# One number in a planner's table: the high half of a piece of the input is ranked earlier in the opening of a transformer block

## The chip, the core and the metric

The kernel runs on one core of a Trainium2 chip. A core has a matrix engine (TensorE, here PE), a vector engine (VectorE, DVE), an engine for activations and copies (ScalarE, ACT), a general one (GpSimd, POOL) and one that here only issues transfers (SyncE, SP). Each works through its own list of instructions in order and waits for the others by semaphores. The metric is the device time of one execution in microseconds, as the median of several runs.

## The reference

A decoder block on 1024 rows of 1024 channels. The opening of the kernel computes the part from `x` to the queries and keys: each row is scaled by the reciprocal root of its mean square, each channel by a gain, and the result is multiplied by the columns of `w_in` that make q and k.

```
def hybrid_layer(h, ..., w_in, ..., mix_pre_g, ...):
    u = rms_norm(h, mix_pre_g)
    z = jnp.einsum('bsd,de->bse', u, w_in)
    p, q, k, v = z[..., :o1], z[..., o1:o2], z[..., o2:o3], z[..., o3:o4]
    gate_a, gate_b = z[..., o4:o5], z[..., o5:]
    ya = pool_mixer(p, ...) @ w_branch_a
    yb = diff_attention(q, k, v, ...) @ w_branch_b
    m = sigmoid(gate_a) * ya + sigmoid(gate_b) * yb
    h = h + rms_norm(m @ w_out, mix_post_g)
    u = rms_norm(h, ffn_pre_g)
    f = silu(u @ w_ffn_gate) * (u @ w_ffn_up)
    return h + rms_norm(f @ w_ffn_down, ffn_post_g)
```

## The kernel before

**Numbers in two halves.** Every matrix operand is split into a high half, its rounding to the matrix engine's format, and a low half, the value minus that rounding. A product is then three matmuls: high by high, high by low, low by high. In most places ACT makes the high half (a CAST row) and DVE the low half (a TENSOR_TENSOR row of line 1405).

**The input in quarters.** The normalised input is kept transposed, channels along the partitions, in four quarters of 512 channels by 512 rows of `x`: A11 and A12 hold rows 0 to 511, A21 and A22 rows 512 to 1023; the second digit of A11/A12 is the channel half. A11 and A12 are prepared in two pieces, rows 0 to 255 and rows 256 to 511. A21 lies in the buffer S1_raw and A22 in S3_raw until sums overwrite them. In names without buffer numbers A11, A12, A21 and A22 are all just `A`, and S1_raw and S3_raw are `S_raw`.

A piece goes through these steps. Line 430 on ACT (or 433 on DVE) scales by the gain, in place or from the loaded buffer; a group of two blocks of 128 rows gets its sums of squares on ACT (line 389, "square"), a mean on DVE (397), a root on POOL (398), a transposition on PE that spreads it over the partitions (404) and a copy into the table `R` (408). Then follows the second stage, `second_stage(n, q, ii)`:

```
pl.op("DVE", dve(size), lambda: tt(a(), a(), Rs()[:, rest]..., ALU.mult), ..., rank=R + OFF[3], port=True)
e = HI[2 * n + q]
o = pl.op(e, act(size) ..., (A.copy ...)(hi2()[:, ks, c], a()), ..., rank=R + OFF[4], ...)
pl.op("DVE", dve(size), lambda: k.sub(lo2()[:, ks, c], a(), hi2()[:, ks, c]), ..., rank=R + OFF[5], port=True)
```

So: multiply by R on DVE (line 303), round on ACT or DVE (line 458, "the rounding"), subtract on DVE (line 1405). `n` is 0 and 1 for the two pieces of A11/A12 and 2 for A21/A22, and `q` the channel half. A21 is done in two halves of 1024 columns, A22 at once with 2048.

**What PE does meanwhile.** Heads 0 and 1 get queries and keys by plain matmuls (line 542): first over rows 0 to 255, then 256 to 511 (128x256 matmuls), then 512 to 1023 (128x512). Head 2 follows by a scheme of seven products (lines 1498 to 1500) on sums S1 to S4 of the quarters, which DVE forms from 2048-column rows, and on differences of the weights (wf_t at line 601, Wh and Wl at lines 591 and 1405). The finished queries and keys go through ACT and DVE (`qk_st`, the high half and the remainder) and out by SP. Fillers that keep PE busy before the first data (`warm`) come first. The rest of the kernel, from about 81 us on, is written in another order of code and its instructions are the same.

**What sets the order.** The opening is planned before anything is emitted. Each step is an operation with an engine, an estimated cost, its predecessors and a rank. `aim` gives each step a due time from the PE step that needs it, and adds the step's own rank to it; `schedule` then goes along the estimated time and gives each engine, of the steps that could start within a short patience (0.1 us for DVE and ACT, none for PE), the one with the lowest rank. On PE, a step that is not yet possible is passed over for one that is. Every later choice depends on the earlier ones. What comes out is a fixed list for each engine; on the chip nothing is reordered. The rank of a piece's steps is its entry in `XT` plus the entry in `OFF` for the kind of step; entry 2n + q belongs to the piece.

Of the kernel before, what the change touches and what calls it, by code (L numbers as in the profile page):

```python
# [257 lines left out]
UNS = ()  # L258
GROUPS = ((0, 1,), (2, 3,), (4, 5,), (6, 7,),)
RT = (10.633, 28.077, 18.684, 6.937,)  # L260
XT = (-25.843, 33.103, -24.124, -5.443, 51.062, -7.924,)
XG = ("DVS", "ACT", "ACT", "ACT", "ACT", "ACT",)
HI = ("ACT", "ACT", "DVE", "ACT", "ACT", "ACT",)
UHI = ("ACT", "ACT",)
# [16 lines left out]
def opening(pl, k):  # L281
# [57 lines left out]
    def pcols(n):  # L339
        return slice(2 * P * n, 2 * P * (n + 1)) if n < 2 else slice(None)  # L340
# [72 lines left out]
    def first_stage(n, q, ii):  # L413
        t = n // 2
        A_, ks, R = RAWS[t, q], slice(2 * ii[0], 2 * ii[-1] + 2), XT[2 * n + q] + .001 * ii[0]
        c, width, nk = pcols(n), 2 * P if t == 0 else HALF, 2 * len(ii)
# [27 lines left out]
    def second_stage(n, q, ii):  # L444
        t = n // 2
        A_, ks, R = RAWS[t, q], slice(2 * ii[0], 2 * ii[-1] + 2), XT[2 * n + q] + .001 * ii[0] + (LATE if n in UNS else 0)
        c, width, nk = pcols(n), 2 * P if t == 0 else HALF, 2 * len(ii)
# [1529 lines left out]
```

## Time and profile before

| | |
|---|---|
| median of 3 runs | 1242.33 us (1241.83 to 1242.55) |
| the profiled execution | 1242.02 us, its span 1240.2 us |
| PE busy | 1231.4 us of the span |
| DVE busy | 844.6 us |
| ACT busy | 584.1 us |
| POOL busy | 126.8 us |
| first 512-wide matmul, first matmul of head 2's scheme | 37.48 us, 59.26 us |

All times within the execution count from the start of the span. A row of the order in time gives start, duration, engine, line, operation, output and inputs, how many equal instructions were merged into it, and in square brackets how long the engine had been idle and whose work ended that. Instructions of one engine overlap a little: the next starts before the last has ended, so what an instruction costs its engine is the distance between two starts. The ends of matmuls are modelled; a busy PE can hide short waits. A row of stretches gives the length, then busy time and count for PE, PEld (weight loads), DVE, ACT and POOL, the granted clock, the share of the transfer engines and GB/s.

### The profile page before, as it was taken

Reading aid. Unit: us, or ns where it says so; the run is one execution under the profiler, and the core shown is the slowest. Engines: PE = TensorE matmul, PEld = TensorE weight load, DVE = VectorE, ACT = ScalarE, POOL = GpSimd, SP = SyncE. Lnnn points to the kernel's source line nnn. Section 1 sums busy time; section 2 is a strip of 40 time slices with the busy share of each in tenths; the row PEclk is TensorE's granted clock in tenths of the full one; section 3 lists DMA queues with packets and bytes.
Section 4 is the critical chain, followed back from the end, with each engine's and each line's share of the span. In section 5 each row is a group of like instructions: output and inputs, shape, how many; then the busy total and the mean of one; then the engine's idle time right before and its main releaser. Section 6 shows DMA issues by size and latency. Waiting matters only on the chain.

```text
span 1240.2 us, 15622 instructions
## 1 busy us (share of the span) xinstructions
PE 1231.4 (99%) x5860; PEld 1034.7 (83%) x5860; DVE 844.6 (68%) x1307; ACT 584.1 (47%) x1049; POOL 126.8 (10%) x108
## 2 busy tenths in 40 slices
PE   9999999999999999999999999999999999999998
PEld 9888888888899998888888888888888888888886
DVE  6986784544599888886885564565655548855666
ACT  8643443443587773454643333333333334454542
POOL 1000000000201110011001111101111101000222
PEclk9999999999999999999999999999999999999999
DMA  9665246423883028663523233232332468633236
GB/s 373 238 194 186 104 166 212 135 73 116 300 310 137 18 86 294 195 241 102 189 90 121 86 127 103 97 98 98 114 127 86 125 225 287 214 102 102 81 106 212
DMA packets 133820, 194.36 MB, mean 157 GB/s; under 512 B 7920, under 2 KB 82416, under 8 KB 131312
## 3 DMA queue, kind: packets, MB, share of 16 engines
q1 hardware_dynamic: 126928, 172.26, 41.5%
q10 hardware_dynamic: 6816, 21.11, 4.4%
q8 instruction: 46, 0.75, 0.2%
q14 instruction: 30, 0.25, 0.1%
HBM read 131.73 MB, written 61.60 MB: 156 GB/s over the span
## 4 chain that ended last, share of the span: by engine, by line
PE 95%; DMA 3%; DVE 1%; ACT 1%; SPq 0%; issue 0%; POOLq 0%; DVEq 0%; ACTq 0%
PE Y L1498 10%; PE Y L1499 10%; PE Y L1500 10%; PE X L1498 5%; PE X L1500 5%; PE X L1499 5%; PE Yd L1498 3%; PE Yd L1499 3%; PE Yd L1500 3%; PE Z L1500 3%; PE Z L1498 3%; PE Z L1499 3%; PE s L710 3%; PE o L710 3%; PE qk L542 3%; PE wo L1500 2%
## 5 line engine op out<-in xcount | busy, mean ns | idle before, releaser
L1449 DVE TENSOR_TENSOR p<-Z,p 128x512 f32<-128x512 f32 x32 | 22.1, 691 | 161.1 <-PE Z L1500 161.1
L1498 PE MATMUL X<-S_hi,Wh 128*128 128x512 f32 x288 | 112.5, 391 | 0.0
L1498 PE MATMUL Y<-S_hi,Wh 128*128 128x512 f32 x288 | 112.4, 390 | 0.0
L1499 PE MATMUL Y<-S_lo,Wh 128*128 128x512 f32 x288 | 112.3, 390 | 0.0
L1500 PE MATMUL Y<-S_hi,Wl 128*128 128x512 f32 x288 | 112.3, 390 | 0.0
L1500 PE MATMUL X<-S_hi,Wl 128*128 128x512 f32 x288 | 112.2, 390 | 0.0
L1499 PE MATMUL X<-S_lo,Wh 128*128 128x512 f32 x288 | 112.2, 390 | 0.0
L1498 PE MATMUL Y<-A_hi,Wh 128*128 128x512 f32 x280 | 109.2, 390 | 0.0
L1499 PE MATMUL Y<-A_lo,Wh 128*128 128x512 f32 x280 | 109.2, 390 | 0.0
L1500 PE MATMUL Y<-A_hi,Wl 128*128 128x512 f32 x280 | 109.1, 390 | 0.0
L1467 ACT CAST Wh<-wf_t 128x1024 fp32r<-128x1024 f32 x62 | 64.3, 1052 | 64.3 <-PE Y L1499 32.9
L1405 DVE TENSOR_TENSOR w_op<-wd,w_op 128x512 fp32r<-128x512 f32 x77 | 56.6, 735 | 53.3 <-ACT w_op L1453 53.2
L1405 DVE TENSOR_TENSOR Wl<-wf_t,Wh 128x1024 fp32r<-128x1024 f32 x72 | 87.6, 1224 | 6.1 <-ACT Wh L1467 4.6
L1453 ACT CAST w_op<-wd 128x512 fp32r<-128x512 f32 x77 | 47.9, 622 | 81.6 <-PE Yd L1500 36.2
L1467 ACT CAST Wh<-w_raw 128x1024 fp32r<-128x1024 f32 (+1 forms) x62 | 51.9, 837 | 63.1 <-PE Z L1499 38.3
L1405 DVE TENSOR_TENSOR Wl<-w_raw,Wh 128x1024 fp32r<-128x1024 f32 x72 | 68.7, 954 | 15.1 <-ACT Wh L1467 13.6
L1498 PE MATMUL Yd<-w_op,s_op 128*128 128x512 f32 x176 | 68.7, 390 | 0.0
L1499 PE MATMUL Yd<-w_op,s_op 128*128 128x512 f32 x176 | 68.6, 390 | 0.0
L1500 PE MATMUL Yd<-w_op,s_op 128*128 128x512 f32 x176 | 68.4, 390 | 0.0
L1498 PEld LDWEIGHTS Y<-S_hi,Wh 128*128 128x128 f32 x288 | 54.1, 188 | 11.6 <-ACT u L1540 0.5
L1500 PEld LDWEIGHTS X<-S_hi,Wl 128*128 128x128 f32 x288 | 54.1, 188 | 11.2
L1500 PEld LDWEIGHTS Y<-S_hi,Wl 128*128 128x128 f32 x288 | 54.1, 188 | 11.2
(294 smaller groups left out, 3025.8 us busy)
## 6 DMA issues: line engine op xcount, KB each, us to landing
s_raw<-fsd SPq DMA_DIRECT2D x35, 512.0 KB, 3.7
w_raw<-in_w_in_dram SPq DMA_DIRECT2D x24, 512.0 KB, 4.2
w_raw<-in_w_ffn_gate_dram SPq DMA_DIRECT2D x22, 512.0 KB, 3.9
w_raw<-in_w_ffn_up_dram SPq DMA_DIRECT2D x22, 512.0 KB, 3.9
fsd<-fss SPq DMA_DIRECT2D x11, 1024.0 KB, 3.9
wd<-in_w_ffn_down_dram SPq DMA_DIRECT2D x44, 256.0 KB, 5.4
fsd<-F SPq DMA_DIRECT2D x33, 256.0 KB, 2.4
sgs<-sgd SPq DMA_DIRECT2D x16, 512.0 KB, 8.5
```

Source lines behind the costliest of these rows:

```text
L542: nc.tensor.matmul(o()[:, cs], l, r, start=first and kk == 2 * kh and j == 0, stop=last and kk == 2 * kh + 1 and j == len(todo) - 1, skip_ ...
L710: nc.tensor.matmul(o, l, r, start=start, stop=stop, skip_group_check=skip)
L1405: nc.vector.tensor_tensor(out=o, in0=a, in1=f32(hi), op=ALU.subtract)
L1449: nc.vector.tensor_tensor(out=o, in0=a, in1=b, op=op)
L1453: nc.scalar.copy(hi, a)
L1467: nc.scalar.copy(hi, a)
L1498: nc.tensor.matmul(o, ah, bh, start=start, stop=False, skip_group_check=goes_on)
L1499: nc.tensor.matmul(o, ah, bl, start=False, stop=False, skip_group_check=goes_on)
L1500: nc.tensor.matmul(o, al, bh, start=False, stop=stop, skip_group_check=goes_on)
```

## The change

One entry of the table `XT` changes: the fourth, n = 1 and q = 1, which is A12's piece of rows 256 to 511. It is lowered by 16.

```
 RT = (10.633, 28.077, 18.684, 6.937,)
-XT = (-25.843, 33.103, -24.124, -5.443, 51.062, -7.924,)
+XT = (-25.843, 33.103, -24.124, -21.443, 51.062, -7.924)
 XG = ("DVS", "ACT", "ACT", "ACT", "ACT", "ACT",)
 HI = ("ACT", "ACT", "DVE", "ACT", "ACT", "ACT",)
```

All steps of that piece get a lower rank: its scaling on ACT, its multiplication, its rounding and its low half. The planner is run again, so everything behind the first different choice may come out otherwise. No instruction is added, removed or resized in the opening.

The lists are equal up to the third of four squares that run in a row on ACT. From there, ACT's list before (numbers behind a name are buffer numbers; `w_raw` are loaded weights, `gk` the gain):

```order
L389 ACTIVATE junk_79,ss_83_413<-xt_49_197 128x1024
L389 ACTIVATE junk_79,ss_83_413<-xt_52_207 128x1024
L458 CAST A12_hi_62_276<-A12_raw_50_199 128x4x256
L430 ACTIVATE S1_raw_53_214<-S1_raw_53_214,gk_36_138 128x512
L430 ACTIVATE S3_raw_55_223<-S3_raw_55_223,gk_36_138 128x512
L430 ACTIVATE S1_raw_53_214<-S1_raw_53_214,gk_36_138 128x512
L430 ACTIVATE S3_raw_55_223<-S3_raw_55_223,gk_36_138 128x512 x3
L515 ACTIVATE qk_st_90_497<-qk_67_297 128x512
```

And ACT's list now, at the same place:

```order
L389 ACTIVATE junk_79,ss_83_413<-xt_49_197 128x1024
L458 CAST A12_hi_62_276<-A12_raw_50_199 128x4x256
L389 ACTIVATE junk_79,ss_83_413<-xt_52_207 128x1024
L430 ACTIVATE S1_raw_53_214<-S1_raw_53_214,gk_36_138 128x512
L430 ACTIVATE S3_raw_55_223<-S3_raw_55_223,gk_36_138 128x512
L430 ACTIVATE S1_raw_53_214<-S1_raw_53_214,gk_36_138 128x512
L430 ACTIVATE S3_raw_55_223<-S3_raw_55_223,gk_36_138 128x512
L515 ACTIVATE qk_st_90_484<-qk_67_297 128x512
L430 ACTIVATE S3_raw_55_223<-S3_raw_55_223,gk_36_138 128x512
L430 ACTIVATE S1_raw_53_214<-S1_raw_53_214,gk_36_138 128x512
L430 ACTIVATE S3_raw_55_223<-S3_raw_55_223,gk_36_138 128x512
```

The rounding of A12's second piece has changed places with the last square; behind that, the last scaling of S3_raw has moved from the sixth place of its row to the eighth, with a qk rounding and a scaling of S1_raw in between.

PE's list where it reaches rows 256 to 511, before (`qk` are accumulators, `w_hi` and `w_lo` weights, `R` and `rstd` the roots' transposition):

```order
L542 MATMUL qk_67_297<-A11_hi_59_252,w_hi_63_280 128x256 x4
L542 MATMUL qk_60_262<-A11_hi_59_252,w_hi_58_239 128x256 x4
L542 MATMUL qk_77_358<-A11_hi_59_252,w_hi_71_323 128x256 x4
L542 MATMUL qk_80_375<-A11_hi_59_252,w_hi_73_331 128x256 x2
L404 MATMUL R_88_453<-ident_72,rstd_85_438 128x128 x2
L542 MATMUL qk_80_375<-A11_hi_59_252,w_hi_73_331 128x256 x2
L542 MATMUL qk_67_297<-A12_hi_62_276,w_hi_63_280 128x256 x2
L404 MATMUL R_89_462<-ident_72,rstd_87_449 128x128 x2
```

And PE's list now, at the same place:

```order
L542 MATMUL qk_67_297<-A11_hi_59_252,w_hi_63_280 128x256 x4
L542 MATMUL qk_60_262<-A11_hi_59_252,w_hi_58_239 128x256 x4
L542 MATMUL qk_67_297<-A12_hi_62_276,w_hi_63_280 128x256 x4
L542 MATMUL qk_67_297<-A11_hi_59_252,w_lo_68_300 128x256 x2
L404 MATMUL R_86_450<-ident_72,rstd_85_439 128x128 x2
L542 MATMUL qk_67_297<-A11_hi_59_252,w_lo_68_300 128x256 x2
L542 MATMUL qk_67_297<-A12_hi_62_276,w_lo_68_300 128x256 x4
L542 MATMUL qk_67_297<-A11_lo_64_282,w_hi_63_280 128x256 x4
L542 MATMUL qk_67_297<-A12_lo_69_313,w_hi_63_280 128x256 x4
L404 MATMUL R_89_476<-ident_72,rstd_88_466 128x128 x2
```

The first use of A12's second piece stands behind 8 matmuls of this part instead of 16; the eight for `qk_77` and `qk_80` come later. The second transposition stands behind all of `qk_67`.

DVE's list from the multiplication of S3_raw by R on, before (`A21_lo` and `A22_lo` are low halves; the second `S1_raw<-S1_raw,R` is A21's second half):

```order
L303 TENSOR_TENSOR S3_raw_55_223<-S3_raw_55_223,R_57_230 128x2048
L518 SCALAR_TENSOR_TENSOR qk_st_90_497<-qk_67_297,qk_st_90_497 128x512
L1405 TENSOR_TENSOR qk_st_93_525<-qk_60_262,qk_st_93_525 128x512
L601 TENSOR_TENSOR wf_t_95_543<-w_raw_78_368,w_raw_65_286 128x512
L601 TENSOR_TENSOR wf_t_95_543<-w_raw_78_368 128x512
L1405 TENSOR_TENSOR A21_lo_97_560<-S1_raw_53_214,A21_hi_91_504 128x1024
L518 SCALAR_TENSOR_TENSOR qk_st_96_556<-qk_77_358,qk_st_96_556 128x512
L303 TENSOR_TENSOR S1_raw_53_214<-S1_raw_53_214,R_57_230 128x1024
```

And DVE's list now:

```order
L518 SCALAR_TENSOR_TENSOR qk_st_90_484<-qk_67_297,qk_st_90_484 128x512
L303 TENSOR_TENSOR S3_raw_55_223<-S3_raw_55_223,R_57_230 128x2048
L1405 TENSOR_TENSOR qk_st_91_509<-qk_60_262,qk_st_91_509 128x512
L601 TENSOR_TENSOR wf_t_95_545<-w_raw_78_368,w_raw_65_286 128x512
L601 TENSOR_TENSOR wf_t_95_545<-w_raw_78_368 128x512
L518 SCALAR_TENSOR_TENSOR qk_st_96_549<-qk_77_358,qk_st_96_549 128x512
L1405 TENSOR_TENSOR A21_lo_98_571<-S1_raw_53_214,A21_hi_93_528 128x1024
L1405 TENSOR_TENSOR A22_lo_101_586<-S3_raw_55_223,A22_hi_97_562 128x2048
L1405 TENSOR_TENSOR qk_st_100_584<-qk_80_375,qk_st_100_584 128x512
L303 TENSOR_TENSOR S1_raw_53_214<-S1_raw_53_214,R_57_230 128x1024
```

A21's second multiplication now stands behind A22's low half of 2048 columns and one more qk remainder. Its rounding on ACT follows it in both, and PE's use of that rounding is the seventeenth 512-wide matmul in both lists. Later, for head 2, the low half of the weights T1 (`Wl` from `wf_t_95`) stands behind the sums S3 and S4 and S3's low half, where before it stood ahead of them.

More of the change, by code (lines that the diff above doesn't have):

```diff
@@ L260 @@
 RT = (10.633, 28.077, 18.684, 6.937,)
-XT = (-25.843, 33.103, -24.124, -5.443, 51.062, -7.924,)
+XT = (-25.843, 33.103, -24.124, -21.443, 51.062, -7.924)
 XG = ("DVS", "ACT", "ACT", "ACT", "ACT", "ACT",)
```

## The prediction

> **What bounds the kernel now.** I read the page's busy shares first, then who TensorE waited for, then its busy time after the opening, then the chain that ended last.
>
> ```profile
> PE 1231.4 (99%) x5860; PEld 1034.7 (83%) x5860; DVE 844.6 (68%) x1307; ACT 584.1 (47%) x1049; POOL 126.8 (10%) x108
> ...
> PE warm L318 <- POOL ident masks.py:199: 1.4, 1, 1.4
> PE qk L542 <- ACT A_hi L458: 1.0, 2, 0.5
> PE branch L1498 <- DVE sgs L713: 0.2, 1, 0.2
> ...
> 110.00:1240.00 1130.00, 1123.84 (x5268) 940.09 (x5266) 754.84 (x1195) 516.99 (x951) 119.75 (x91) 1.00 0.44 146
> ...
> 26.58 0.94 ACT A_hi L458
> 28.28 31.14 PE qk L542 x174
> ```
>
> TensorE (PE) works 99% of the span. From 110 us on it idles 6.2 of 1130 us, 0.2 of it in a wait at line 1498 and the rest behind its last matmul. So a microsecond that PE loses in the opening should come out at the end, and one saved there too. Of the opening's two waits for a rounding (line 458, 1.0 us together), the second is the one in the chain, at 26.58, and is the one that the change speaks to. These are its rows on PE, with the places that I need later, and then those on ScalarE (ACT):
>
> ```profile
> 24.78 1.84 PE L542 MATMUL qk<-A_hi,w_hi 128*128 128x256 f32 x14
> 26.59 0.48 PE L542 MATMUL qk<-A_hi,w_hi 128*128 128x256 f32 x2
> 27.57 0.50 PE L542 MATMUL qk<-A_hi,w_hi 128*128 128x256 f32 x2 [0.49 <-ACT A_hi L458]
> 37.48 1.32 PE L542 MATMUL qk<-A_hi,w_hi 128*128 128x512 f32 x5
> 41.13 1.52 PE L542 MATMUL qk<-A_hi,w_hi 128*128 128x512 f32 x6
> 59.26 0.39 PE L1498 MATMUL Y<-A_hi,Wh 128*128 128x512 f32 x1
> ```
>
> ```profile
> 24.23 1.06 ACT L389 ACTIVATE junk<-xt 128x1024 bf16<-128x1024 f32 x1
> 25.43 1.06 ACT L389 ACTIVATE junk<-xt 128x1024 bf16<-128x1024 f32 x1
> 26.48 1.03 ACT L458 CAST A_hi<-A_raw 128x1024 fp32r<-128x1024 f32 x1
> 27.42 3.79 ACT L430 ACTIVATE S_raw<-S_raw,gk 128x512 f32<-128x512 f32 x6
> 31.11 0.58 ACT L515 ACTIVATE qk_st<-qk 128x512 fp32r<-128x512 f32 x1
> 31.59 1.04 ACT L458 CAST A_hi<-S_raw 128x1024 fp32r<-128x1024 f32 x1
> ...
> 36.19 1.90 ACT L458 CAST A_hi<-S_raw 128x2048 fp32r<-128x2048 f32 x1
> ...
> 38.94 1.06 ACT L458 CAST A_hi<-S_raw 128x1024 fp32r<-128x1024 f32 x1 [0.37 <-DVE S_raw L303]
> ```
>
> PE issues a 256-wide matmul every 0.12 us (24.78 to 26.46 or so for 14), so the pair at 26.59 would have been followed at 26.83; it was followed at 27.57, 0.06 after the rounding ended at 27.51. Lost: 0.74. The 512-wide ones come every 0.227 us: 16 from 37.48 to 41.13, and 80 from there to 59.26.
>
> **The change part by part.** *The rounding moves ahead of one square.* A rounding follows a square's start by 1.05 (25.43 to 26.48). Behind the third square, which starts at 24.23 as before, that is 25.28, and the end 26.31 instead of 27.51: 1.20 earlier. PE can go on at 26.37.
>
> *PE's order moves with it.* It now asks for this rounding behind 8 of the matmuls at 24.78 instead of behind 16: at 24.78 + 8 x 0.12 = 25.74. It loses 26.37 - 25.74 = 0.63 instead of 0.74. The first gain is thus 0.11 us and not 0.74, since the eight matmuls that covered the wait now stand behind it; no instruction is added or removed on PE.
>
> *The square itself ends later.* It starts 0.94 after the rounding (26.48 to 27.42), at 26.22, and ends at 27.28 instead of 26.49. Behind it wait its mean on VectorE (DVE), the root on POOL, the transposition on PE, now placed 20 matmuls behind the wait (some 29.1, with 0.3 for each pair of transposes), the copy of R, and S1's first multiplication. By the DVE row at 29.53 below, that one was not late before; at some 29.8 to 30.1 it ends by 31.3 and the qk remainder behind it by 31.9. DVE then has to wait for ACT anyway, until 32.2 (next step), so all this costs nothing. Should the copy of R come later than 30.4, that cover is gone and the excess adds to the sum.
>
> *ACT's scalings spread out, and with them a DVE wait.* Before, DVE's large S3 multiplication started when the sixth scaling ended.
>
> ```profile
> 29.53 1.23 DVE L303 TENSOR_TENSOR S_raw<-S_raw,R 128x1024 f32<-128x1024 f32 x1
> 31.24 2.29 DVE L303 TENSOR_TENSOR S_raw<-S_raw,R 128x2048 f32<-128x2048 f32 x1 [0.48 <-ACT S_raw L430]
> 33.45 0.68 DVE L518 SCALAR_TENSOR_TENSOR qk_st<-qk,qk_st 128x512 fp32r<-128x512 f32 x1
> 34.09 0.69 DVE L1405 TENSOR_TENSOR qk_st<-qk,qk_st 128x512 fp32r<-128x512 f32 x1
> 34.69 0.68 DVE L601 TENSOR_TENSOR wf_t<-w_raw,w_raw 128x512 f32<-128x512 f32 x1
> 35.29 0.69 DVE L601 TENSOR_TENSOR wf_t<-w_raw 128x512 f32<-128x512 f32 x1
> 35.89 1.22 DVE L1405 TENSOR_TENSOR A_lo<-S_raw,A_hi 128x1024 fp32r<-128x1024 f32 x1
> 37.03 0.69 DVE L518 SCALAR_TENSOR_TENSOR qk_st<-qk,qk_st 128x512 fp32r<-128x512 f32 x1
> 37.63 1.22 DVE L303 TENSOR_TENSOR S_raw<-S_raw,R 128x1024 f32<-128x1024 f32 x1
> ...
> 41.77 2.29 DVE L1405 TENSOR_TENSOR A_lo<-S_raw,A_hi 128x2048 fp32r<-128x2048 f32 x1
> 43.97 2.29 DVE L303 TENSOR_TENSOR S_raw<-S_raw,S_raw 128x2048 f32<-128x2048 f32 x1
> ```
>
> Six scalings took 0.615 each (27.42 to 31.11). The first now starts 1.05 to 1.20 behind the square at 26.22 (both distances stand in the rows: to a rounding, to another square), so at 27.27 to 27.42; I take 27.3, nearest to the first. The last of S3 is now the eighth item: six scalings and one qk rounding of 0.48 (31.11 to 31.59) run ahead of it, 27.3 + 3.69 + 0.48 = 31.47, and it ends 0.71 later at 32.18. DVE starts 0.03 later (31.21 to 31.24): 32.21 instead of 31.24. The one load that this scaling order asks for earlier than before is S1's second half:
>
> ```profile
> L353 SPq DMA_DIRECT2D S_raw<-in_xt_dram x1: 328/328/328, 20.3 to 20.3; - x1
> DMA to landing us min/median/max: 10.2/10.2/10.2
> ```
>
> It lands at 30.5; its scaling comes up at 27.3 + 5 x 0.615 + 0.48 = 30.85. Loads on SP keep their order up to there, so none is late; later seats of SP, and POOL's, feed work tens of us ahead of its use.
>
> *S1's second half falls behind A22's low half on DVE.* This is the largest term. Before, its multiplication at 37.63 led to the rounding at 38.94 to 40.00, and PE asked for that at 41.13: 1.1 us to spare. Now DVE runs ahead of it, from 32.21: the S3 multiplication 2.21, four small ones of 0.60, A21's low half 1.14, A22's low half of 2048 columns 2.20 (41.77 to 43.97), one small one 0.60. That is 8.55, so it starts at 40.76, ends 1.22 later at 41.98, ACT rounds from 42.07 (0.09, as from 38.85 to 38.94) to 43.13, and PE goes on at 43.19. ACT holds none of this up, but narrowly: from 31.47 its list has two scalings, two qk roundings and a half-width weight of about 0.48 each, two roundings of 0.94 and A22's of 1.90, and is through at 37.9; DVE takes up A22's low half at 37.96. PE asks at about 41.1 as before. So a wait of 2.1 us opens, and PE is late by 43.19 - 41.13 = 2.06 against before, whatever was won at 26 us: time won there only lengthens this wait.
>
> *Sum.* -0.11 at the first wait, +2.17 at the second: +2.06, up to +2.2 with the later first scaling; I take +2.1. The profiled execution took 1242.02 (its span 1240.2 and 1.8 around it), 0.3 below the runs' median of 1242.33. On the first that gives 1244.1, on the median 1244.4, which I forecast.
>
> Does a 2.1 us pause also slow what follows? Before, PE ran its first, 128-wide transposes slower than the later ones:
>
> ```profile
> 6.00:7.00 1.00, 1.00 (x6) 1.00 (x5) 0.00 (x0) 1.00 (x2) 0.00 (x0) 1.00 1.04 426
> 7.00:8.00 1.00, 1.00 (x11) 1.00 (x10) 0.17 (x1) 0.86 (x4) 0.68 (x1) 1.00 1.00 387
> ```
>
> Six in one microsecond, eleven in the next, while the granted clock reads 1.00 in both. The 0.5 us wait at 27 us brought no such slow stretch. I therefore put no cost on it in the sum, and the slow start as a rival. The Trainium skill ("TensorE: Matmul & The Clock Gate", Part 1) says that the matrix clock drops to half once PE has been idle for about one window of 3.4 us; by that rule 2.1 us fall short and the sum stays, and no run here shows a pause of this length.
>
> **The rivals.** *A: PE falls back to its slow start.* From 1.4 to 7.0 us, 5.6 us, it ran at 6/11 of its rate; as much again behind the pause would cost 5.6 x 5/11 = 2.5 us: 1246.9. For it speaks that the pause is four times any shown; against, that the ones shown left no trace and the cited rule. 6%.
>
> *B: a second wait, at T1's low half.* Head 2's low half of T1 on DVE moves from behind the qk remainders to behind S4 and S3's low half.
>
> ```profile
> 55.38 0.60 ACT L515 ACTIVATE qk_st<-qk 128x512 fp32r<-128x512 f32 x1 [2.83 <-PE qk L542]
> ```
>
> From 40.76 DVE has S1's half (1.13), two of 0.60, two of 1.14, four of 2.20, two of 0.60 and S3's sum: 57.6. Then it waits for this rounding, 2.06 later than before and thus over at 58.04, and goes on with 0.60, 2.20, 2.20 and T1's 1.22: 64.3. PE wants it at the 15th matmul behind 59.26 + 2.06, at 64.5. Only 0.2 to spare behind twenty instructions: were each 0.03 slower, PE would wait 0.4 more, 1244.8. The DVE rows vary by less than 0.01, which speaks against. 14%.
>
> *C: not slower.* The 2.1 us come back later, in the attention stage, where the chain goes through transfers:
>
> ```profile
> 469.53 7.24 DMA sgs<-sgd
> ...
> 481.13 11.04 DMA sgs<-sgd
> ```
>
> If PE is paced there by transfers that do not start later when PE is late, and the waits are hidden under the modelled ends of matmuls, it could swallow the delay: 1242.3. It decides from 2.1 us of hidden waiting. The one wait shown there is 0.2 (line 1498), and the buffers these transfers fill are freed by the delayed work. 6%. That the change does not take place is excluded by the order.
>
> **How the numbers follow.** 72% for the forecast, 1244.0 to 1244.9 by itself; 14, 6 and 6% for B, A and C; 2% for a gain that I cannot name. The range, 1243.6 to 1245.4, holds the forecast and B, reaches 0.8 below and 1.0 above for hand-overs, which I know to 0.1 each, and leaves out A and C. 0.2%, about 2.5 us, is what a measurement of this kernel tells from no change. So the forecast counts as the same, but 0.4 us more makes it slower: 11 of its 72%, 10 of B's 14 and all of A give 27% slower; 71% the same; 2% faster.
>
> **What would show it.** PE's wait at line 458 near 26 us shrinks only to about 0.45 as the profile counts it, and starts a microsecond earlier. A new one of about 2 us stands at 41 us, ended by ACT's rounding of S_raw, with DVE's half-width S_raw multiplication at 40.8 and its 2048-wide A_lo ahead of it. The first Y matmul moves from 59.26 to about 61.3, and no further wait follows. I am wrong if DVE reaches that multiplication before 39, if PE's matmuls behind 43 us come at more than 0.227, or if a wait at T1 appears at 64.

## The result and the profile after

| | before | changed |
|---|---|---|
| median, us | 1242.57 (14 runs) | 1245.07 (14 runs, 1244.4 to 1246.2) |
| ratio, 95% interval | 1 | 1.0023, 1.0016 to 1.0030 |
| the profiled execution, us (its span) | 1242.02 (1240.2) | 1245.14 (1243.3) |

One run of the kernel before, at 1365.71 us, was disturbed and is not in the ratio. The change costs 2.5 us by the medians and 2.9 us by the ratio. That is within the predicted range of 1243.6 to 1245.4, but the whole interval lies above 1, and the ratio above the 0.2% that the prediction took as its border: the kernel is slower, where I had given "the same" 71%.

Who TensorE waited for, of the changed kernel (total, times, longest):

```profile
PE qk L542 <- ACT A_hi L458: 2.5, 4, 1.1
...
PE qk L542 <- DVE qk_st L1405: 1.1, 1, 1.1
PE Y L1498 <- DVE p L1449: 0.5, 1, 0.5
PE R L404 <- POOL rstd L398: 0.2, 1, 0.2
```

Before, there were only the waits for `A_hi` (1.0) and the 0.2 at line 1498, and the fillers' 1.4, which is the same now. The 0.2 for a root stands at 7.96 us, ahead of the first place where the lists differ. Two lines are new that the prediction did not have: a wait for a low half of `qk`, and one for a sum `p`. Their places are in TensorE's rows of the changed kernel (start, duration, and in brackets the idle time before the row):

```profile
24.33 1.12 PE L542 MATMUL qk<-A_hi,w_hi 128*128 128x256 f32 x8
26.53 0.74 PE L542 MATMUL qk<-A_hi,w_hi 128*128 128x256 f32 x4 [1.08 <-ACT A_hi L458]
...
37.59 1.32 PE L542 MATMUL qk<-A_hi,w_hi 128*128 128x512 f32 x5
...
39.65 0.39 PE L542 MATMUL qk<-A_hi,w_lo 128*128 128x512 f32 x1
41.15 0.50 PE L542 MATMUL qk<-A_hi,w_hi 128*128 128x512 f32 x1 [1.11 <-DVE qk_st L1405]
41.48 0.39 PE L542 MATMUL qk<-A_lo,w_hi 128*128 128x512 f32 x1
```

```profile
43.41 1.66 PE L542 MATMUL qk<-A_hi,w_hi 128*128 128x512 f32 x6 [0.61 <-ACT A_hi L458]
...
61.69 0.39 PE L1498 MATMUL Y<-A_hi,Wh 128*128 128x512 f32 x1
...
97.68 0.50 PE L1498 MATMUL Y<-A_hi,Wh 128*128 128x512 f32 x1 [0.47 <-DVE p L1449]
```

Laid against the rows before, matmul by matmul, TensorE is 0.1 us late at 37 us (37.59 against 37.48), 2.3 us late at 43 us (43.41 against 41.13), 2.4 at the first Y (61.69 against 59.26), still 2.4 at 94 us, and 3.1 behind the wait at 97.68 (that matmul stood at 94.62 before). With the restart it is 3.2, it moves between 2.9 and 3.2 in the attention stage, and the end is 3.1 us later. So the loss has two places, 41 to 43 us and 97 us. Each restart behind a wait also costs 0.1: the next 512-wide matmul comes after 0.33 us (41.15 to 41.48) instead of 0.227.

At the first place, VectorE's and ScalarE's rows of the changed kernel show the order that the prediction described, a quarter of a microsecond later than it said:

```profile
32.41 2.29 DVE L303 TENSOR_TENSOR S_raw<-S_raw,R 128x2048 f32<-128x2048 f32 x1 [0.43 <-ACT S_raw L430]
...
37.02 3.48 DVE L1405 TENSOR_TENSOR A_lo<-S_raw,A_hi 128x1024 fp32r<-128x1024 f32 x2
40.41 0.68 DVE L1405 TENSOR_TENSOR qk_st<-qk,qk_st 128x512 fp32r<-128x512 f32 x1
41.01 1.22 DVE L303 TENSOR_TENSOR S_raw<-S_raw,R 128x1024 f32<-128x1024 f32 x1
```

```profile
42.31 1.05 ACT L458 CAST A_hi<-S_raw 128x1024 fp32r<-128x1024 f32 x1 [3.67 <-DVE S_raw L303]
```

The row at 37.02 holds A21's low half (1024 columns) and A22's (2048). Behind it come the low half of `qk` at 40.41 and then S1's multiplication. The first stop, at 39.9, is for that low half: it reads the PSUM bank into which TensorE wants to put head 1's next product. The second, six matmuls later, is the predicted one for the rounding at 42.31.

At 97 us the sums of head 3 stand behind differences of the weights of a later unit. VectorE of the kernel before, and then of the changed one:

```profile
89.38 0.69 DVE L1449 TENSOR_TENSOR p<-Z,p 128x512 f32<-128x512 f32 x1 [1.89 <-PE Z L1500]
...
91.31 0.69 DVE L1449 TENSOR_TENSOR wf_t<-w_raw,w_raw 128x512 f32<-128x512 f32 x1 [0.64 <-DMA w_raw<-in_w_in_dram]
...
93.12 0.68 DVE L1449 TENSOR_TENSOR p<-Y,p 128x512 f32<-128x512 f32 x1
```

```profile
92.72 0.69 DVE L1449 TENSOR_TENSOR wf_t<-w_raw,w_raw 128x512 f32<-128x512 f32 x1 [1.17 <-DMA w_raw<-in_w_in_dram]
...
93.93 0.68 DVE L1449 TENSOR_TENSOR p<-Z,p 128x512 f32<-128x512 f32 x1
...
95.13 0.69 DVE L1449 TENSOR_TENSOR wf_t<-w_raw,wf_t 128x512 f32<-128x512 f32 x1
...
96.34 0.68 DVE L1449 TENSOR_TENSOR wf_t<-w_raw,wf_t 128x512 f32<-128x512 f32 x1
96.94 0.68 DVE L1449 TENSOR_TENSOR p<-Y,p 128x512 f32<-128x512 f32 x1
```

Before, `p<-Z` ran at 89.38, ahead of the difference that waits for a weight load, and `p<-Y` ended at 93.80, 0.8 us before TensorE wanted that bank of `Y` again. Of the unit's four weight differences, two stood ahead of `p<-Y` (91.31 and 92.52) and two behind it (from 93.72). Now two stand ahead of `p<-Z`, where they wait for the load until 92.72, and the other two stand between the sums, at 95.13 and 96.34. `p<-Y` ends at 97.62, and TensorE goes on at 97.68, where 97.05 would have been its next start. The last two differences cost VectorE 1.2 us; by an estimate from these rows, `p<-Y` would have ended near 96.4 without them, in time in spite of the load. The chain of work that ended last says the same: in the changed kernel it goes through the multiplication and rounding at 41 and 42 us, and through the load.

```profile
41.09 1.15 DVE S_raw L303
42.31 1.05 ACT A_hi L458
...
86.28 6.35 DMA w_raw<-in_w_in_dram
```

### The profile page after: what moved, and what is told of

Read it like the earlier page. It is cut to its first block, busy times and chain, and to the rows that moved or that the text cites. A ratio compares the mean times of both kernels' runs of the same rounds, so it can differ in the third digit from the quotient of the medians.

```text
span 1243.3 us, 15626 instructions
## 1 busy us (share of the span) xinstructions
PE 1231.5 (99%) x5860; PEld 1032.4 (83%) x5860; DVE 845.0 (68%) x1307; ACT 584.6 (47%) x1049; POOL 126.4 (10%) x108
## 4 chain that ended last, share of the span: by engine, by line
PE 94%; DMA 2%; DVE 1%; ACT 1%; issue 1%; SPq 0%; POOLq 0%; DVEq 0%; ACTq 0%
PE Y L1498 10%; PE Y L1500 10%; PE Y L1499 10%; PE X L1498 5%; PE X L1500 5%; PE X L1499 5%; PE Yd L1499 3%; PE Yd L1498 3%; PE Yd L1500 3%; PE s L710 3%; PE Z L1500 3%; PE Z L1498 3%; PE Z L1499 3%; PE o L710 3%; PE branch L1498 2%; PE branch L1500 2%
```

## The experiments

Most kernels below move steps in the list that the planner has made, just before it is emitted. `move(engine, step, of)` takes a step of an engine's list, by its number there, and puts it ahead of another; with `True` behind it.

```diff
     first.schedule(OPENING_PATIENCE, BEGIN)
+    def move(engine, step, of, behind=False, on=None):
+        mine = [t for t in first.order if t.engine == engine]
+        t, o = mine[step], [t for t in first.order if t.engine == (on or engine)][of]
+        first.order.remove(t)
+        first.order.insert(first.order.index(o) + behind, t)
...
```

Behind the opening the framework sets the order anew, from its own estimate, so such a move can also change the order at 97 us. Where it does, the text says so.

### Is the stop at 41 us VectorE's order? The order of before in the changed kernel (e1)

```diff
+    move("DVE", 44, 47, True)
+    move("DVE", 44, 45, True)
+    move("DVE", 40, 45, True)
+    move("DVE", 40, 41, True)
```

> The changed kernel, with VectorE's list from the 38th to the 46th us in the order of the kernel before: the second S1 multiplication, then the low half of qk (128x512), then the low half of A21's second part, and A22's low half behind them; the rounding on ScalarE stays ahead of the square. Theory (the loss at 41 us lies in VectorE's order alone): the two stops of TensorE of 1.11 and 0.61 us at 41 and 43 us shrink to under 0.3 us together, the first Y matmul comes at about 59.7 us instead of 61.69, and the time is about 1242.8 us, 0.2 to 0.3 over the kernel before. Behind the opening the sum p<-Z stands ahead of the weight differences again in this kernel, so the wait at 97 us should be gone too; if it is not, 1243.5. Rival (the later start of the scalings on ScalarE sets the stop): the stop stays at about 2 us and the time near 1244.4.

Measured: 1242.45 us against 1242.15 for the kernel before in the same series, ratio 1.0003 (0.9994 to 1.0012). TensorE and VectorE at the place:

```profile
39.75 0.39 PE L542 MATMUL qk<-A_hi,w_lo 128*128 128x512 f32 x1
40.12 0.50 PE L542 MATMUL qk<-A_hi,w_hi 128*128 128x512 f32 x1
...
59.74 0.39 PE L1498 MATMUL Y<-A_hi,Wh 128*128 128x512 f32 x1
```

```profile
38.24 1.22 DVE L303 TENSOR_TENSOR S_raw<-S_raw,R 128x1024 f32<-128x1024 f32 x1
39.38 0.68 DVE L1405 TENSOR_TENSOR qk_st<-qk,qk_st 128x512 fp32r<-128x512 f32 x1
```

The stop shrinks to 0.14 us (40.12 - 39.75 - 0.227), the first Y stands at 59.74 as expected, and the wait at 97 us is gone, since the framework puts `p<-Z` ahead of the differences again. The exchange on ScalarE, and what it moved on TensorE and POOL, are still in this kernel. With VectorE in the old order all that costs 0.3 us by the medians, which the interval does not tell from nothing; the rest of the loss comes by way of VectorE's order. A small wait of the kind of rival B shows here: VectorE ends T1's low half at 64.08, TensorE goes on with it at 64.14, and the distance to the kernel before grows from 0.48 to 0.74 us.

### The same from the other side: VectorE's new order in the kernel before (e4)

```diff
+    move("DVE", 45, 40)
+    move("DVE", 41, 42, True)
```

> The kernel before, with only VectorE's order changed to that of the changed kernel around 38 us: A22's low half and then the low half of qk ahead of the second S1 multiplication. ScalarE and TensorE keep their lists. Theory: TensorE stops at about 40 us for 1.1 us (for VectorE's qk_st) and behind it for about 0.7 us (for ScalarE's A_hi); the first Y comes at about 61.5 us instead of 59.26, and the time is 2.1 to 2.4 over the kernel before, about 1244.8 us, without a wait at 97 us. Rival (the loss is in what ScalarE's swap delays): no more than 0.3 us, about 1242.7. Rival (a pause brings slower matmuls behind it): more than 3.5 us, over 1246.

Measured: 1244.41 us against 1242.15, ratio 1.0017 (1.0008 to 1.0026).

```profile
41.33 0.50 PE L542 MATMUL qk<-A_hi,w_hi 128*128 128x512 f32 x1 [1.14 <-DVE qk_st L1405]
...
43.59 1.66 PE L542 MATMUL qk<-A_hi,w_hi 128*128 128x512 f32 x6 [0.61 <-ACT A_hi L458]
```

The same two stops, with ScalarE and TensorE on their old lists, and no wait at 97 us. 2.3 us of the changed kernel's loss are thus made by two steps, A22's low half and `qk`'s, standing ahead of S1's second multiplication. The first Y came at 61.88, 0.4 later than I expected, for the two restarts and a prefix of the program 0.3 later.

### Is the wait at 97 us the order or the load? (e2)

```diff
-        tt(t13[:, 0], u[:, 0], g[:, 0], ALU.subtract)
-        tt(t13[:, 1], u[:, 1], u[:, 0], ALU.subtract)
+        for d in tt(t13[:, 0], u[:, 0], g[:, 0], ALU.subtract), tt(t13[:, 1], u[:, 1], u[:, 0], ALU.subtract):
+            if len(units) == 1:
+                tc.add_manual_dep(d.ins, adds[1].ins.name, ..., reason="behind the first unit's sums")
+        units.append(t13)
...
+            adds.append(tt(o, acc, t, ALU.add))
```

> The changed kernel with one order between two steps of VectorE added: the first two weight differences of the second unit behind the opening come behind the first unit's sums p<-Z and p<-Y, as in the kernel before; the load they wait for stays as late as it is. Theory (0.77 us of the loss is TensorE's wait at 97.7 us for the sum behind the late load): this wait goes, the stops at 41 and 43 us stay, and the time is 0.6 to 0.8 below the changed kernel's, about 1244.3 us. Rival (the load is what is late, so the wait only moves to the weights of that unit): the same 1245.1 us as the changed kernel, with a wait on Wh or Wl behind 97 us.

Measured: 1244.15 us against 1242.15, ratio 1.0016 (1.0007 to 1.0025). The changed kernel's own ratio was 1.0023, so the gain is about 0.9 us, though the intervals overlap; the trace decides. The stops of this kernel on TensorE, and `p<-Y` on VectorE:

```profile
26.15 0.74 PE L542 MATMUL qk<-A_hi,w_hi 128*128 128x256 f32 x4 [0.60 <-ACT A_hi L458]
...
40.76 0.50 PE L542 MATMUL qk<-A_hi,w_hi 128*128 128x512 f32 x1 [1.10 <-DVE qk_st L1405]
...
43.02 1.66 PE L542 MATMUL qk<-A_hi,w_hi 128*128 128x512 f32 x6 [0.60 <-ACT A_hi L458]
```

```profile
94.13 0.69 DVE L1449 TENSOR_TENSOR p<-Y,p 128x512 f32<-128x512 f32 x1 [0.63 <-PE Y L1505]
```

These are all the stops that its profile shows between 24 and 100 us. The sum `p<-Y` now waits for TensorE instead of the other way round, and no wait on `Wh` or `Wl` follows: the weight load has time to spare, and only the differences put ahead of the sums made it a wait. The edit names the first two; the other two come behind them, from 95.94 us.

### The exchange on ScalarE alone (e5, and the same kernel again as e5b and e5c)

```diff
+    move("ACT", 30, 31, True)
```

> The kernel before, with only ScalarE's swap: the rounding of A12's second part ahead of the last square, all other lists as before. Theory (the rounding comes 1.05 us earlier, but TensorE now meets the transposition of the last rows' root, which comes 1.05 us later): the wait for A_hi at 27 us goes, a wait of about 1.7 us for rstd takes its place, TensorE is 0.6 to 0.8 us later from 29 us on, no stop at 41 us, and the time is about 1243.2 us. Rival (the swap itself brings the loss of the changed kernel): 1244.5 or more. Rival (the wait for the rounding was the only one that counted): a gain of 0.5 or more, under 1242.1.

> The kernel of e5 once more, for another profiled execution. Theory (the halved clock behind its stop of 2.5 us comes in some executions and not in others, and is what spreads its times from 1243.0 to 1245.9 us): without the slow stretch the time is 1242.9 to 1243.8 us, with it 1244.3 to 1245.9 us. Rival (the spread has another cause): a time in one of these groups with the other group's clock.

> The kernel of e5 a third time, with the same expectation: a slow stretch of 3.4 us with a time of 1244.3 to 1245.9 us, or none with 1242.9 to 1243.8 us; any other pairing speaks for another cause.

Measured: a median of 1244.35 us against 1242.15, ratio 1.0015 (1.0006 to 1.0024), and in the two further executions 1242.88 and 1244.31 against 1241.96. The median is a microsecond over my number, and the first eleven runs fall in two groups: five from 1242.95 to 1243.75 with a mean granted clock of 0.999, six from 1244.35 to 1245.87 with 0.997 or 0.998. The three profiles show what parts them. The transposition that TensorE stops for, in the first, second and third:

```profile
29.38 0.43 PE L404 MATMUL R<-ident,rstd 128*128 128x128 f32 x2 [2.22 <-POOL rstd L398]
```

```profile
29.02 0.43 PE L404 MATMUL R<-ident,rstd 128*128 128x128 f32 x2 [1.51 <-POOL rstd L398]
```

```profile
29.18 0.43 PE L404 MATMUL R<-ident,rstd 128*128 128x128 f32 x2 [2.07 <-POOL rstd L398]
```

And their two stretches of 3.4 us from 27.4 us on (length, busy time of PE with its count, of the weight loads and the other engines, then the granted clock), in the same order:

```profile
27.40:30.80 3.40, 1.42 (x12) 1.42 (x13) 2.15 (x5) 3.40 (x7) 1.60 (x1) 0.98 1.03 410
30.80:34.20 3.40, 3.40 (x18) 3.40 (x18) 3.40 (x3) 1.70 (x3) 0.00 (x0) 0.52 0.83 329
```

```profile
27.40:30.80 3.40, 1.89 (x16) 1.78 (x16) 2.23 (x4) 3.39 (x6) 1.57 (x1) 1.00 1.02 408
30.80:34.20 3.40, 3.40 (x30) 3.40 (x30) 3.40 (x3) 2.70 (x5) 0.00 (x0) 1.00 0.98 383
```

```profile
27.40:30.80 3.40, 1.61 (x13) 1.62 (x14) 2.23 (x5) 3.40 (x6) 1.60 (x1) 0.96 1.03 408
30.80:34.20 3.40, 3.40 (x19) 3.40 (x19) 3.40 (x3) 1.81 (x4) 0.00 (x0) 0.54 0.82 323
```

Behind a stop of 2.2 or 2.1 us the clock is half for the next 3.4 us, 18 or 19 matmuls run there instead of 30, and TensorE loses 1.5 us more (30 matmuls take 5.16 us instead of 3.68); behind the stop of 1.5 us nothing of the kind happens. The first profile's 1245.87 holds besides a wait of 0.77 us for a transfer in the attention stage, at 492.75, which the other two do not have. So the exchange taken alone does not bring the changed kernel's stop at 41 us (none of the three has it), but a wait of its own for the root, as expected, and this wait is long enough to change the clock in some executions.

I had expected a stop of about 1.7 us. The root took 0.9 us longer than in the kernel before in all three, and the rows say why. The root on POOL and the subtraction on VectorE in the first of them:

```profile
27.55 1.22 DVE L1405 TENSOR_TENSOR A_lo<-A_raw,A_hi 128x1024 fp32r<-128x1024 f32 x1
```

```profile
27.73 1.60 POOL L398 TENSOR_TENSOR rstd<-ms,mhalf 128x2 f32<-128x2 f32 x1 [1.57 <-DVE ms L397]
```

The root takes 1.60 us and ends 0.56 behind the subtraction (29.33 and 28.77). In the changed kernel, where the subtraction is over by then (26.51 to 27.73), it takes 0.70:

```profile
27.89 0.70 POOL L398 TENSOR_TENSOR rstd<-ms,mhalf 128x2 f32<-128x2 f32 x1 [1.65 <-DVE ms L397]
```

In the kernel before, the root ran from 26.86 to 27.56, and the subtraction began at 27.54, held back by the rounding. The swap left the subtraction where it was, at 27.55, and brought the root 0.9 us later, onto it.

### How long a pause slows the clock

Sums on an unused tile, which compute nothing that is used, ahead of `qk`'s low half in the changed kernel: two of them (e7), then six (e10).

```diff
+    low = [t for t in first.order if t.engine == "DVE"][41]
+    for _ in range(2):
+        first.order.insert(first.order.index(low), Task("DVE", 0.0, lambda: nc.vector.tensor_tensor(
+            out=junk, in0=junk, in1=junk, op=ALU.add), 0.0, 0.0))
```

> The changed kernel with two sums of 128x1024 on an unused tile put ahead of the low half of qk on VectorE (they compute nothing that is used), so that TensorE's first stop at 41 us grows from 1.1 to about 3.3 us; everything behind it is later by the same 2.2 us. Theory (the halved clock seen in e5 behind a pause of 2.5 us depends on the length of the pause, so here it comes in nearly every execution): a granted clock of about 0.5 for some 3.4 us behind the stop, matmuls of 512 columns every 0.43 us instead of 0.227, and 1.5 to 1.8 us on top of the pause: about 1248.2 us. Rival (a pause costs its own length alone, as in the changed kernel): about 1246.7 us, the granted clock 1.00 behind it.

> The changed kernel with six of the sums on the unused tile (0.67 us each in e7) ahead of qk's low half, so that the stop at 41 us grows from 1.1 to about 5.1 us. Theory (a granted clock of half follows where one activity window of about 3.4 us is mostly idle, wherever it begins): with a stop longer than a window every execution has it, for one window of 3.4 us: 4.0 us of pause and 1.5 to 1.8 us of slow matmuls over the changed kernel, so about 1250.4 us by the kernel before of this series at 1242.4. Rival (pauses cost their length alone, and what slowed e5 was something else there): about 1248.8 us, granted clock 1.00 behind the stop.

Measured with two: 1247.00 us against 1242.57, ratio 1.0038 (1.0025 to 1.0050). The tile is of 16 bit and a sum took 0.67 us, so the stop grew by 1.3 us, not by 2.2; the pause alone then gives 1246.4 (the changed kernel's 1245.07 and 1.3) to 1246.7 (by its ratio). In the profiled execution it was just that:

```profile
42.60 0.50 PE L542 MATMUL qk<-A_hi,w_hi 128*128 128x512 f32 x1 [2.41 <-DVE qk_st L1405]
```

```profile
43.00:46.40 3.40, 2.79 (x13) 1.95 (x12) 3.37 (x5) 2.22 (x3) 0.00 (x0) 1.00 0.41 154
```

The clock stayed at 1.00 behind a stop of 2.4 us, longer than those of 2.1 and 2.2 that halved it above. So length alone does not decide, and my theory that nearly every execution would have it was wrong at this length. Of the other four executions one took 1246.50 us at a mean granted clock of 0.999, and three took 1247.00, 1247.75 and 1247.77 at 0.997 or 0.998; in these the clock may have fallen, which no trace shows.

Measured with six: 1249.89 us against 1241.96, ratio 1.0064 (1.0050 to 1.0077), near the 1250.4 of the theory and 1.1 above the rival (both counted from 1242.4 for the kernel before; by the difference, 7.9 us, it is 0.1 under the theory and 1.5 over the rival). Its stretches of 3.4 us, laid at the places where the clock changes:

```profile
39.30:42.70 3.40, 0.64 (x3) 0.19 (x1) 3.30 (x5) 0.00 (x0) 0.00 (x0) 1.00 0.41 158
42.70:46.10 3.40, 0.82 (x2) 0.73 (x3) 3.33 (x5) 0.00 (x0) 0.00 (x0) 0.50 0.00 0
46.10:49.50 3.40, 3.40 (x9) 2.63 (x9) 3.37 (x5) 2.64 (x3) 0.00 (x0) 0.50 0.41 154
49.50:53.00 3.50, 3.50 (x16) 2.89 (x16) 3.43 (x3) 1.09 (x2) 0.00 (x0) 0.99 0.54 150
```

The clock falls 2.9 us into the stop, while TensorE still stands, and stays at half for two stretches of 3.4 us, the second of them fully busy. A stretch in which TensorE was mostly idle is followed each time by one at half clock.

The traces also hold the times at which the granted clock changed, and these show where such stretches lie. In all thirteen traces every later change comes a whole number of steps of 3.413 us behind the first change to full speed: the fall in the first profile of the exchange alone 23.893 us behind it (7 steps), the one with six sums 37.547 (11 steps), the one at the end of the kernel before 1232.211 (361 steps). So the windows are fixed within an execution, and they lie differently in each: the first change comes between 4.1 and 7.5 us. TensorE's idle time in these windows, with the modelled ends of matmuls, and the clock of the window behind:

| execution | window, us | idle in it, us | clock of the next |
|---|---|---|---|
| six sums | 39.30 to 42.71 | 2.77 (81%) | half |
| six sums, the next one | 42.71 to 46.12 | 2.57 (75%) | half |
| exchange alone, first | 27.24 to 30.66 | 2.14 (63%) | half |
| exchange alone, third | 27.12 to 30.54 | 2.07 (61%) | half |
| two sums | 41.18 to 44.59 | 1.76 (52%) | full |
| the changed kernel with the differences behind the sums | 39.57 to 42.98 | 1.65 (48%) | full |
| exchange alone, second | 27.93 to 31.34 | 1.09 (32%) | full |
| the changed kernel | 38.27 to 41.68 | 1.11 (33%) | full |

These rows fit one rule: the idle time within one window decides, with a border between 52 and 61%. An edge cut the stop of 2.41 us into 0.99 and 1.42, and the one of 1.51 into 0.42 and 1.09. The two stops of the changed kernel are 1.72 us together, half of a window at most, so by this they stay below the border wherever the windows lie.

### What the exchange could be worth

The kernel before with the exchange on ScalarE, A12's low half ahead of the mean on VectorE, and the root's transposition, its copy and S1's first multiplication moved behind 24 or more matmuls of A12 (e6); in the second (e8) also `qk`'s high and low halves ahead of A22's rounding and of S1's second multiplication; in the third (e9) the transposition four matmuls earlier (132 in place of 134).

```diff
+    move("ACT", 30, 31, True)
+    move("DVE", 29, 28)
+    move("DVE", 32, 134, True, "PE")
+    move("DVE", 30, 134, True, "PE")
+    move("PE", 123, 134, True)
...
+    move("ACT", 46, 47, True)
+    move("DVE", 40, 41, True)
```

> The kernel before with the rounding ahead of the last square, and the transposition of the last rows' root moved behind 24 matmuls of A12 on TensorE (its copy and the first S1 multiplication on VectorE with it, A12's low half ahead of the mean); VectorE keeps the order of the kernel before around 38 us. Theory (the swap pays only where no root and no bank waits behind it): TensorE's wait of 0.5 us for the rounding at 27 us shrinks to nothing and it is 0.6 to 0.7 us early from 28 us on; at 39 us it then meets the low half of qk, which VectorE ends at 39.4 to 39.5 us as in the kernel before, and gives 0.4 to 0.5 back; the time is 0.1 to 0.3 below the kernel before, about 1242.0 us. Rival (the wait at 27 us was all that counted): 0.7 below, 1241.45. Rival (the later first S1 multiplication passes on): 0.3 or more over, 1242.5.

> e6, with two more exchanges at 37 us: ScalarE rounds qk (128x512) ahead of A22, VectorE takes qk's low half ahead of the second S1 multiplication. Theory (in e6 the gain is given back to the bank of qk): the bank's wait goes, the second rounding of S1 comes at about 40.5 us, 0.1 to 0.3 us behind TensorE, and the time is 0.3 to 0.5 below the kernel before, about 1241.75 us. Rival (ScalarE, idle until qk is done, delays the roundings behind it): a wait of 0.5 or more for A_hi at 40 us and no gain against e6, 1242.0 or more.

> e8 with the root's transposition (and its copy and the first S1 multiplication) four matmuls earlier, behind the low half of A12. Theory (in e6 and e8 the gain of 0.7 us at 27 us was given back because the root came late, so that VectorE ended qk's low half of the other head after TensorE wanted its bank): the first S1 multiplication comes at about 30.0 us instead of 30.5, the stop of 0.54 us at 38 us shrinks to under 0.1, and the time is 0.4 to 0.7 below the kernel before, about 0.5 below e8. Rival (something else keeps VectorE late): the stop stays at 0.4 or more and the time is that of the kernel before.

Measured: 1242.69 and 1242.76 us against 1242.57 (ratios 1.0000, 0.9991 to 1.0009, and 1.0001, 0.9992 to 1.0010), and 1242.13 against 1241.96 (1.0003, 0.9994 to 1.0012). None beats the kernel before by what can be measured; the expected gains of 0.1 to 0.7 us did not come. In all three the wait for the rounding at 27 us is gone. In the first two the gain goes to another bank, that of the other head's `q`, for whose low half TensorE stops at 38 us; of the second:

```profile
38.10 0.50 PE L542 MATMUL qk<-A_hi,w_hi 128*128 128x512 f32 x1 [0.54 <-DVE qk_st L518]
```

In the third this stop is down to about 0.25 us, not under 0.1 as expected, and TensorE is 0.6 us early behind 41 us, of which it was 0.4 early at 24 us already, ahead of the moved steps. By 490 us, in the attention stage, 0.3 is left of that in the profiled execution, and the median shows nothing. None of these three orders keeps the 0.7 us from 27 us; what takes it back is a bank each time, and in the third then also the attention stage.

## Why the prediction was wrong, point by point

- **The first wait.** Right in kind: it was not removed by the exchange, since TensorE's list asks for the rounding eight matmuls earlier. The experiment on the load at 97 us (e2) shows the wait at 0.60 us where I gave about 0.45; in the changed kernel's own profile it is 1.08, because TensorE reached it 0.45 earlier in that execution. TensorE stood 0.1 late behind it instead of 0.1 early.
- **The square, the root and the scalings.** Right. S3's multiplication waited for ScalarE until 32.41 (32.21 predicted), the copy of R and S1's first multiplication cost nothing. The first scaling began at 27.43, at the upper end of what I gave, and I took the lower. The rows before show 0.13 and 0.14 us for a pair of transposes (26.46 to 26.59, 27.90 to 28.04), not the 0.3 that I used; that cost nothing.
- **S1's second half behind A22's low half on VectorE.** The mechanism is right, and the two experiments on VectorE's order show it from both sides. The size was off: TensorE went on at 43.41 instead of 43.19, for the 0.2 us by which the scalings were late, and lost 0.1 more in the restart. Where I had it late by 2.06 us it was late by 2.28, and by 2.42 behind the restart. I had not seen that the same order stops TensorE twice; the bank of `qk` alone would have cost 1.3 us, but it lies inside the wait that I had counted, which ends with the rounding whenever TensorE comes, so this miss cost nothing.
- **"No further wait follows" and "later seats of SP, and POOL's, feed work tens of us ahead of its use".** This is the step that failed. A wait of 0.77 us with its restart follows at 97.7 us. I had looked at VectorE's list up to T1 and at the transfers of the opening, and not at the order that the framework makes behind it, where two weight differences that wait for a load had moved ahead of both sums, and two more ahead of the sum that frees a bank. That the change reaches there could be read from the order; that the place had 0.8 us to spare before, and a load that VectorE waited 0.64 us for, stood in the trace.
- **The rivals.** B (a wait at T1's low half) did not come in the changed kernel: T1's low half started at 63.45 and TensorE passed it without a wait. It showed, with 0.26 us, where VectorE kept the old order (e1). C (swallowed in the attention stage) fell: of a delay of 3.2 us behind 97.7 us, 3.1 are left at the end. A (a slow clock behind the pause) did not come in the profiled execution, where the matmuls behind 43 us keep their 0.227; but my reason for 6% was too good. The Trainium skill ("TensorE: Matmul & The Clock Gate", Part 1) puts the fall to half clock behind about one idle window of 3.4 us, and I let 2.1 us fall short of it. The experiment with ScalarE alone shows the fall behind 2.1 us. The page also says that the windows run free of the program. There the runs agree, with steps of 3.413 us; they differ in that a window 61% idle was enough. The changed kernel's stops, half a window at most, stay under that; I had the right outcome for a reason that does not hold. One window at half clock cost 1.5 us in the exchange alone, not the 2.5 of the rival. The 1.00 that I read for the slow first matmuls says nothing: the record of the clock begins with the change to full speed at 7.07 us, where the rate goes from six to eleven a microsecond.
- **The sum.** -0.11 and +2.17 were forecast; the profiled execution shows +0.11 at the first wait, +2.31 at the second and +0.77 at 97 us, less 0.1 behind it: +3.1. All three differences push to the side of "slower", to which I gave 27%.
- **The border between "same" and "slower".** I took 0.2%, about 2.5 us, as what a measurement tells from no change. By that border it is the wait at 97 us that made the kernel slower: without it the ratio is 1.0016. But the interval of the result reaches only 0.07%, 0.9 us, to each side, and the kernels of e2 and e4, 2.0 and 2.3 us over the kernel before, have their whole intervals above 1. My own +2.1 us would have shown as slower too, so 71% for "the same" was also too much for the sum that I had.

## What to carry to other kernels

A step moved in one engine's list moves others in all lists, and the loss is made where the later list reaches a bank or a buffer: follow the list of every engine up to the next point at which an order is set anew, and then one unit beyond. A gain at a wait is worth no more than the slack at the next bank behind it, here nothing in two orders and 0.4 us of 0.7 in the third. And give a new pause of about 2 us a real chance of a slower clock behind it, since whether it comes depends on how the windows lie in the execution.

## What the runs showed of the hardware

- The matrix clock changed only in whole steps of 3.413 us, which lie differently in each execution. It fell to half for a window behind one in which TensorE was idle for 2.07 us or more (61% and more), and did not behind one with 1.76 us (52%). A fall cost the exchange alone 1.5 us, and that kernel's first eleven times fell into two groups, 1242.95 to 1243.75 and 1244.35 to 1245.87.
- A root of 128x2 on POOL took 0.70 us where no subtraction ran on VectorE and 1.60 where one of 1.22 us had begun 0.2 us earlier, and ended 0.55 to 0.56 behind it in all three profiles of the exchange alone. The Trainium skill ("SBUF — State Buffer", "SBUF: two separate sides") says that the two engines share a port pair which one holds for a whole instruction while the other is blocked, also where VectorE reads two inputs from SBUF and the other engine reads there too; these rows agree.
- The first distance between 512-wide matmuls behind a stop at full clock was 0.33 or 0.34 us instead of 0.227. With this and the modelled end of the matmul before it, a wait costs more than it is counted: the one counted as 0.47 us at 97.68 delayed what follows by 0.77.
